# Later places for convolution taps, value-block transposes and LayerNorm in a two-group decoder layer

## The chip, the core and the metric

The kernel runs on one core of one Trainium2 chip. The metric is the device time of one execution in microseconds (us). The core has five engines that work side by side: TensorE (PE in the rows, PEld for its weight loads), VectorE (DVE), ScalarE (ACT), GpSimd (POOL) and SyncE (SP), which issues the transfers. Each engine takes its instructions from its own queue in the order of the program.

## The reference

One layer of a hybrid causal decoder, for a prompt of 2048 tokens and 8 samples of 8 tokens (64 more tokens) that share every weight. Model width 1024, FFN width 2816.

```python
h = RMSNorm(x)
u = h @ w_in      # columns: conf_val 512 | conf_gate 512 | q k v 3*512 | z 512 | beta 4 | a 4
# Conformer group (512 channels): GLU -> causal depthwise conv (31 taps) -> LayerNorm -> swish
# Gated DeltaNet group (4 heads of 128): short conv (4 taps) + SiLU on q, k, v; q and k L2-normed;
#   chunked delta rule (chunks of 64, a triangular solve, then a scan over chunks);
#   per-head RMSNorm * SiLU(z)
x = x + concat(conformer, deltanet) @ w_out
x = x + W_down(SiLU(gate) * val)    # [gate|val] = causal depthwise conv (3) of RMSNorm(x) @ w_up
x = x + (p @ w_ple) * sigmoid(x @ w_ple_gate)
y = RMSNorm(x)
```

The outputs are y for prompt and samples, and the new convolution and delta-rule states of both.

## The kernel before

The tokens are cut into six passes of 2, 3, 3, 3, 3 and 2 tiles of 128 tokens; the last pass carries the 64 sample tokens too. Channels lie on partitions and tokens along the free dimension, so an operation on pass 0 is 128x256 and one on passes 1 to 4 is 128x384. Every weight is split into two parts of a shorter number format, so that each block of a product is three matmuls (`gemm`, PE rows `g<-hT,w`, `g<-mx,w`, `g<-fbuf,w`).

The work is written as a list of units, each with a place (a number), and the list is sorted by place. `units_b` makes the units of the mixing half of a pass: `conf_gate` (GLU of one channel block, with a tanh of ScalarE, row `t<-g`, that reads the projection's accumulator), the convolution taps (31 per block of 128 channels, each one VectorE multiply-add, rows `cacc<-H,cfS,cacc`), `dn_block(j)` (projection, short conv and SiLU of one q, k or v block; j from 8 to 11 are the four value blocks; its last operation is the VectorE row `y<-t,y`, on a tanh of ScalarE, `t<-y`), `dn_tail(j)` (for a value block: transposes of y on TensorE, rows `m<-ident,y`, and a VectorE product with `irk`), `z_block`, the inversion of the triangular blocks (VectorE rows `tv` and `H<-H,tv`; its `tv` and every tanh take turns in the same three buffers `t`), the scan over chunks (`v_new`, `state`, then `out_a` and `out_b`), LayerNorm (`ln_a`, `ln_b`) and `swish`. `units_mx` splits the mixed result into its two parts (rows `mx<-H`, `mx<-zs`) for the product with w_out.

Passes 0 and 1 share the blocks of w_in: their units are sorted together in the joint stage (about 0 to 293 us), whose places run from 0 to 28 and come from `joint_places`. The rest of the mixing of pass 1 lies beside the FFN of pass 0. From then on, the mixing of pass p+1 lies beside the FFN of pass p: `merge` threads its units, at the fractions 0 to 1 that `usual_places` gives, through those of `units_f` (rows of `gate` and `val` read hT, rows of `down` read fbuf). The FFN of passes 1, 2, 3 and 4 runs at 746 to 1200, 1282 to 1716, 1798 to 2236 and 2318 to 2755 us; each is followed by the product with w_out (`proj`) of the pass after it.

The list is not the last word. A scheduler takes the units in the order of the list, plays them against a timeline of its own, and writes the order of each engine's queue. Where an instruction stands is therefore read from the queues, and not from the places.

Helpers hide the callers' lines in the rows: L89 is every matmul, L93 every transpose, L96 every multiply-add with a per-partition scalar, L100 and L102 operations with a scalar, L105 operations on two tensors, L108 every ScalarE operation.

Of the kernel before, what the change touches and what calls it, by code (L numbers as in the profile page):

```python
# [42 lines left out]
def step_kernel(  # L43
# [36 lines left out]
    def gbank():  # L80
        return pg.tile([P, 512], F32, tag="g", name=nm("g"))
# [25 lines left out]
    def act(out, in_, f=AF.Copy, **kw):  # L107
        A.activation(out, in_, f, **kw)  # L108
# [38 lines left out]
    def r_tile(tag, w=NMAX, dt=F32):  # L147
        return rp.tile([P, w], dt, tag=tag, name=nm(tag), bufs=3)

    def srow_tile():  # L150
        return rp.tile([P, NSQ, 38], F32, tag="srow", name=nm("srow"), bufs=2)
# [275 lines left out]
    def units_b(q, pl):  # L427
# [9 lines left out]
        def take(key):  # L437
            if second and key in hold:
                return hold.pop(key)
            w = get()  # L440
            if first and key not in alone:
                hold[key] = w
            return w

        def add(place, f, *keys):
            out.append((place, keys, f))
# [2 lines left out]
            pass  # L449

        z = St()

        def sm(tag, last=H):
            return dp.tile([P, NG, last], F32, tag=tag, name=nm(tag), bufs=2 if tag in LIVE else 1)
# [35 lines left out]
        def dn_block(j):  # L490
            dnS, qk = W["dn"], z.qk
            w = take(("w_in", D + j * P))
            row = r_tile("row", NMAX + 3)
            y = qk[:, 4 + j if j < 4 else j - 4, :] if j < 8 else r_tile("y")
            srow = srow_tile() if sam else None
            G.tensor_copy(row[:, 0:3], dnh[:, j, 0:3])
            if sam:
                G.tensor_copy(srow[:, :, 0:3], dnS[:, j, 4:28].rearrange("p (s r) -> p s r", r=3))
            ps = gbank()
            gemm_w(ps[:, :n], w, q.hT, 0, n)  # L500
            to_row(q, row, srow, 3, ps, lambda o, i, *a: act(o, i))
            act(y[:, :n], ps[:, :n], scale=dnS[:, j, 3:4])
            G.tensor_copy(dnh[:, j, 0:3], row[:, np_:np_ + 3])
            if sam:
                G.tensor_copy(dnh[:, j, 3:27].rearrange("p (s r) -> p s r", r=3), srow[:, :, 8:11])
            for tap in (2, 1, 0):
                for o, i in taps(q, y, row, srow, tap):
                    stt(V, o, i, dnS[:, j, tap:tap + 1], o, MUL, ADD)
            th = t_tile()
            act(th[:, :n], y[:, :n], AF.Tanh)  # L510
            stt(V, y[:, :n], th[:, :n], 1.0, y[:, :n], ADD, MUL)
            if j >= 8:
                z.y = y

        def dn_tail(j):
            if j < 8:
                y = z.qk[:, 4 + j if j < 4 else j - 4, :]
                ss = z.ssq if j < 4 else z.ssk
                ps = bank()
                sq = t_tile("sq")  # L520
                act(sq[:, :n], y[:, :n], AF.Square)
                for t, c0, L in tiles:
                    mm(ps[:L, t:t + 1], sq[:, c0:c0 + L], one1[:, 0:1], t == 0, t == len(tiles) - 1)
                V.tensor_copy(ss[:, 0:nt, j % 4], ps[:, 0:nt])
                if sam:
                    V.tensor_copy(ss[:NSAM, nt:nt + 1, j % 4], ps[:NSAM, nt:nt + 1])
            else:
                h, y = j - 8, z.y
                ps = bank()
                for t in range(nt):  # L530
                    trn(ps[:, t * P:(t + 1) * P], y[:, t * P:(t + 1) * P])
                tt(V, z.vtk[:, 0:nt, h * P:(h + 1) * P], ps[:, :nt * P].rearrange("p (t c) -> p t c", c=P),
                   bc(z.irk[:, 0:nt, h], P, 2), MUL)
                if sam:
                    ps = bank()
                    trn(ps[:NSAM, :P], y[:, np_:n])
                    ts(V, z.vts[:, h * P:(h + 1) * P], ps[:NSAM, :P], z.irk[:NSAM, nt, h:h + 1], MUL)
# [511 lines left out]
        for (what, j), p in pl.at.items():  # L1049
            if what == "cv":  # L1050
                add(p, lambda j=j: conf_val(j), *keys("w_in", j * P))
            elif what == "cg":
                add(p, lambda j=j: conf_gate(j), *keys("w_in", CW + j * P))
            elif what == "dn":
                add(p, lambda j=j: dn_block(j), *keys("w_in", D + j * P))
                add(p + pl.tail, lambda j=j: dn_tail(j))
            elif what == "z":
                add(p, lambda j=j: z_block(j), *keys("w_in", 2560 + j * P))
        spread(staged(units[0] + units[1], [decay]), *pl.decay)
# [16 lines left out]
        if sam:  # L1076
            p = pl.smp
# [15 lines left out]
    def usual_places(g0, g1):  # L1093
        pl = Places()
        seq = [("cv", 3), ("cg", 3), ("dn", 4), ("cv", 0), ("cg", 0), ("dn", 5), ("dn", 6), ("cv", 1), ("cg", 1),
               ("dn", 7), ("cv", 2), ("cg", 2)] + [("dn", j) for j in (0, 1, 2, 3, 8, 9, 10, 11)] + [
                   ("z", h) for h in range(H)]
        dg = (g1 - g0) / len(seq)
        pl.begin = g0 - 0.02
        pl.at = {("ba", 0): g0 - 0.019}  # L1100
        pl.at.update({k: g0 + dg * i for i, k in enumerate(seq)})
        dn = [pl.at["dn", j] for j in range(12)]
        pl.tail = 0.9 * dg
        pl.soft, pl.eg = g0 + 0.01, g0 + 0.03
        pl.decay = (g0 + 0.05, dn[5])
        pl.k_norm = [dn[j] + 1.3 * dg for j in (5, 7)]
        pl.gram_k = [(dn[j] + 1.6 * dg, dn[j] + 2.6 * dg) for j in (5, 7)]
        pl.gram_q = [(dn[j] + 1.6 * dg, dn[j] + 2.6 * dg) for j in (1, 3)]
        pi = dn[7] + 2.7 * dg
        pl.inv = (pi, pi + 0.03, pi + 0.15)  # L1110
        pl.q_norm = dn[3] + 2.7 * dg
        p = pl.at["cg", 3] + dg
        cuts = [p + (0.86 - p) * x for x in (0, 0.2, 0.42, 0.70, 1.0)]
        pl.conv = [(b, max(cuts[i], pl.at["cg", b] + dg), cuts[i + 1]) for i, b in enumerate((3, 0, 1, 2))]
        pl.smp = dn[3] + 2.8 * dg
        pl.scan = (max(g1 + 0.01, pi + 0.19), 0.965)
        pl.ln, pl.swish = (0.87, 0.92), (0.925, 0.96)
        return pl

    def joint_places(second):  # L1120

        pl = Places()
        seq = [("ba", 0)] + [("dn", j) for j in (4, 5, 6, 7)] + [("cv", 1), ("cg", 1)] + [
            ("dn", j) for j in (8, 9, 10, 11)] + [("cv", 2), ("cg", 2)] + [("dn", j) for j in (0, 1, 2, 3)] + [
                ("z", h) for h in range(H)]
        own = [("cv", 3), ("cg", 3), ("cv", 0), ("cg", 0)]
        lag = 0.4 if second else 0.0
        pl.at = {k: 4 + i + lag for i, k in enumerate(seq)}
        pl.at.update(zip(own, (25, 26, 27, 28) if second else (0, 1, 2, 3)))
        pl.begin = 3.8 if second else -0.5  # L1130
        pl.tail = 0.9
        pl.soft, pl.eg = 5.5 + lag / 2, 6.0 + lag / 2
        pl.k_norm = [7.3 + lag, 9.2 + lag]
        if second:
            pl.decay = (100.0, 100.07)
            pl.gram_k = [(100.03, 100.09), (100.09, 100.14)]
            pl.gram_q = [(100.16, 100.22), (100.22, 100.28)]
            pl.inv = (100.145, 100.18, 100.32)
            pl.q_norm = 100.3
            pl.conv = [(b, 100.14 + 0.17 * i, 100.31 + 0.17 * i) for i, b in enumerate((1, 2, 3, 0))]  # L1140
            pl.scan = (100.36, 100.965)
            pl.ln, pl.swish = (100.85, 100.91), (100.915, 100.95)
        else:
            pl.decay = (6.3, 8.5)
            pl.gram_k = [(7.6, 8.6), (9.5, 10.5)]
            pl.inv = (10.7, 11.7, 16.5)
            pl.gram_q = [(19.6, 20.6), (21.6, 22.6)]
            pl.q_norm = 22.7
            pl.conv = [(3, 2.0, 7.0), (0, 7.0, 12.0), (1, 12.0, 17.0), (2, 17.0, 22.0)]
            pl.scan = (17.6, 27.5)  # L1150
            pl.ln, pl.swish = (22.3, 25.0), (25.0, 26.5)
        return pl


# [249 lines left out]
    def even(units, p0, p1):  # L1404
        return [(p0 + (p1 - p0) * i / len(units), *u) for i, u in enumerate(units)]

    u0, u1 = units_b(ps_[0], joint_places(False)), units_b(ps_[1], joint_places(True))
    joint = u0 + [u for u in u1 if u[0] < 49] + even(units_a(ps_[1]), 0.1, 3.8) + [(1.6, (), small)]
    um = units_mx(ps_[0])
    joint += even(um[0:4], 26.6, 27.4) + even(um[4:8], 27.6, 28.4) + [(22.8, (), load_ffn)]  # L1410
    joint.sort(key=lambda u: u[0])
    plan = units_a(ps_[0]) + [u[1:] for u in joint]
    for ip, q in enumerate(ps_):
# [17 lines left out]
        else:  # L1431
            back = [(u[0] - 100, *u[1:]) for u in u1 if u[0] >= 100.14] if prev is None else units_b(
                nxt, usual_places(0.04, 0.55))
            um = units_mx(nxt)
# [36 lines left out]
```

## Time and profile before

| | us |
|---|---|
| median of 3 runs | 3140.59 |
| lowest, highest | 3140.39, 3149.44 |
| the profiled execution | 3149.25 |
| its span, first to last instruction | 3147.5 |

The mean granted clock of TensorE was 0.974 of full speed. In the rows, busy time is the time in which an engine worked; the idle time before an instruction has behind it the work that ended the wait. The profiled execution is one near the highest of the three times.

### The profile page before, as it was taken

The numbers are of one execution on the slowest core, as the hardware profiler recorded it, in microseconds if no ns is written. First come the engines' busy times: TensorE is split into PE (matmuls) and PEld (weight loads), VectorE is DVE, ScalarE is ACT, GpSimd is POOL, SyncE is SP. The second block draws the span as 40 slices with busy tenths as digits, with TensorE's granted clock in tenths as the row PEclk, the third lists the DMA queues.
The fourth block names the chain that finished last, engine by engine and source line by source line (L and its number), as shares of the span: only waits on it lengthen the run. The fifth ranks groups of instructions, "written<-read, shape, count | busy, mean of one in ns | idle before, by whom it ended". The sixth has DMA issues, their size and how long they took to land.

```text
span 3147.5 us, 50438 instructions
## 1 busy us (share of the span) xinstructions
PE 2966.5 (94%) x18418; PEld 2886.3 (92%) x18418; DVE 2144.5 (68%) x5378; ACT 1093.1 (35%) x2440; POOL 810.3 (26%) x1485
## 2 busy tenths in 40 slices
PE   5979889787999999999999999999999999998998
PEld 5979788787998999999999999999999999998998
DVE  6996889756778685668557656857577866743444
ACT  3434334434232443422234332233342222423223
POOL 3422454334323431311111211111131211111221
PEclk8989899888999999999999999999999999998999
DMA  7646788587777767666756677665767775666886
GB/s 229 200 131 203 241 253 249 191 289 271 259 248 248 256 232 253 248 240 237 244 202 225 227 255 248 233 227 199 253 239 256 259 241 199 224 231 227 293 297 215
DMA packets 300414, 745.25 MB, mean 237 GB/s; under 512 B 51241, under 2 KB 213546, under 8 KB 225023
## 3 DMA queue, kind: packets, MB, share of 16 engines
q1 hardware_dynamic: 300167, 742.03, 69.1%
q8 instruction: 146, 2.39, 0.3%
q14 instruction: 101, 0.83, 0.1%
HBM read 607.75 MB, written 134.57 MB: 236 GB/s over the span
## 4 chain that ended last, share of the span: by engine, by line
PE 63%; DVE 8%; DMA 5%; ACT 1%; issue 1%; SPq 0%; POOL 0%; DVEq 0%; ACTq 0%; POOLq 0%
PE g L89 56%; PE d L89 3%; DMA w<-halves 3%; PE m L89 2%; DVE h L96 1%; PE d L93 1%; DVE y L96 1%; PE m L93 1%; DVE cacc L96 1%; DVE X L100 0%; DVE hT L105 0%; DVE rt L105 0%; DVE H L96 0%; DVE tv L105 0%; DVE zs L105 0%
## 5 line engine op out<-in xcount | busy, mean ns | idle before, releaser
L89 PE MATMUL g<-hT,w 128*128 128x384 f32 (+2 forms) x9048 | 1580.3, 332 | 35.6 <-DMA w<-halves 11.9
L89 PEld LDWEIGHTS g<-hT,w 128*128 128x128 f32 x9048 | 1499.4, 191 | 44.9 <-ACT hT L108 10.8
L89 PE MATMUL g<-fbuf,w 128*128 128x384 f32 (+2 forms) x2904 | 534.9, 334 | 21.8 <-ACT w L108 8.4
L96 DVE SCALAR_TENSOR_TENSOR y<-row,ffS,y 128x384 f32<-128x384 f32 (+1 forms) x528 | 321.5, 609 | 296.5 <-ACT y L108 271.3
L89 PEld LDWEIGHTS g<-fbuf,w 128*128 128x128 f32 x2904 | 477.9, 189 | 31.5 <-DVE X L105 11.2
L96 DVE SCALAR_TENSOR_TENSOR cacc<-H,cfS,cacc 128x384 f32<-128x384 f32 (+1 forms) x696 | 452.8, 651 | 10.6 <-ACT cacc L108 3.7
L105 DVE TENSOR_TENSOR X<-X,g 128x384 f32<-128x384 f32 (+2 forms) x532 | 277.3, 525 | 238.6 <-PE g L89 236.4
L108 ACT ACTIVATE row<-g 128x384 f32<-128x384 f32 (+1 forms) x336 | 152.7, 455 | 640.7 <-PE g L89 639.2
L105 POOL TENSOR_TENSOR w<-raw,w 128x1024 fp32r<-128x1024 f32 x90 | 223.9, 2488 | 183.9 <-ACT w L108 169.8
L1237 POOL COPY ffh<-row 128x2 f32<-128x2 f32 x264 | 57.7, 218 | 638.2 <-ACT row L108 633.3
L89 PE MATMUL g<-x,w 128*128 128x384 f32 (+2 forms) x1152 | 201.7, 328 | 5.7 <-ACT w L108 4.4
L89 PE MATMUL g<-mx,w 128*128 128x384 f32 (+2 forms) x1152 | 193.9, 328 | 9.7 <-DMA w<-halves 8.7
L89 PEld LDWEIGHTS g<-mx,w 128*128 128x128 f32 x1152 | 187.8, 192 | 11.3 <-issue 4.8
L89 PEld LDWEIGHTS g<-x,w 128*128 128x128 f32 x1152 | 189.7, 193 | 6.5 <-ACT w L108 4.8
L1230 POOL COPY row<-ffh 128x2 f32<-128x2 f32 x264 | 79.9, 303 | 432.0 <-DVE y L96 328.6
L108 ACT ACTIVATE y<-g,ffS 128x384 f32<-128x384 f32 (+2 forms) x264 | 169.1, 641 | 0.0
L105 POOL TENSOR_TENSOR fbuf<-y,fbuf 128x384 fp32r<-128x384 f32 (+2 forms) x132 | 135.2, 1024 | 110.8 <-ACT fbuf L108 108.7
L108 ACT ACTIVATE fbuf<-y 128x384 fp32r<-128x384 f32 (+2 forms) x132 | 65.8, 498 | 213.0 <-DVE y L105 212.7
L89 PE MATMUL g<-hf,w 128*128 128x256 f32 x528 | 128.0, 398 | 10.9 <-DMA w<-in_w_up_dram 7.1
L108 ACT ACTIVATE w<-raw 128x1024 fp32r<-128x1024 f32 x106 | 112.0, 1056 | 55.0 <-PE g L89 24.2
L108 ACT ACTIVATE y<-y 128x384 f32<-128x384 f32 (+2 forms) x132 | 65.7, 498 | 187.0 <-DVE y L96 186.5
L89 PEld LDWEIGHTS g<-hf,w 128*128 128x128 f32 x528 | 103.7, 202 | 26.1 <-issue 4.4
(344 smaller groups left out, 3384.2 us busy)
## 6 DMA issues: line engine op xcount, KB each, us to landing
w<-halves SPq DMA_DIRECT2D x477, 1024.0 KB
halves<-w SPq DMA_DIRECT2D x106, 1024.0 KB
raw<-in_w_up_dram SPq DMA_DIRECT2D x44, 512.0 KB
w<-in_w_up_dram SPq DMA_DIRECT2D x33, 512.0 KB
raw<-in_w_in_dram SPq DMA_DIRECT2D x24, 512.0 KB
raw<-in_w_down_dram SPq DMA_DIRECT2D x22, 512.0 KB
xt<-in_x_prompt_dram SPq DMA_DIRECT2D x16, 512.0 KB
xT<-xt SPq DMA_DIRECT2D x16, 512.0 KB
```

The lines of the kernel that those rows point to most:

```text
L89: T.matmul(out, lhsT=lhsT, rhs=rhs, start=start, stop=stop, skip_group_check=skip)
L93: T.transpose(out, in_, ident[:k, :k])
L96: return e.scalar_tensor_tensor(out=out, in0=in0, scalar=scalar, in1=in1, op0=op0, op1=op1)
L105: e.tensor_tensor(out=out, in0=a, in1=b, op=op)
L108: A.activation(out, in_, f, **kw)
L1230: G.tensor_copy(row[:, 0:2], ffh[:, col, 0:2])
L1237: G.tensor_copy(ffh[:, col, 0:2], row[:, np_:np_ + 2])
```

## The change

Three sets of places are other numbers, and one variable becomes a dictionary. No instruction is added or taken away.

```diff
         z = St()
+        z.y = {}
...
             if j >= 8:
-                z.y = y
+                z.y[j] = y
...
-                h, y = j - 8, z.y
+                h, y = j - 8, z.y.pop(j)
...
                 add(p, lambda j=j: dn_block(j), *keys("w_in", D + j * P))
-                add(p + pl.tail, lambda j=j: dn_tail(j))
+                add(p + (pl.tail if j < 8 else pl.vtail), lambda j=j: dn_tail(j))
...
-        pl.tail = 0.9 * dg
+        pl.tail, pl.vtail = 0.9 * dg, 1.4 * dg
...
-        cuts = [p + (0.86 - p) * x for x in (0, 0.2, 0.42, 0.70, 1.0)]
+        cuts = (0.25, 0.43, 0.58, 0.72, 0.86)
...
-        pl.tail = 0.9
+        pl.tail, pl.vtail = 0.9, 1.3
...
-            pl.conv = [(3, 2.0, 7.0), (0, 7.0, 12.0), (1, 12.0, 17.0), (2, 17.0, 22.0)]
+            pl.conv = [(3, 2.0, 8.0), (0, 8.0, 13.5), (1, 13.5, 19.0), (2, 19.0, 24.0)]
...
-            pl.ln, pl.swish = (22.3, 25.0), (25.0, 26.5)
+            pl.ln, pl.swish = (24.2, 26.2), (26.2, 27.2)
...
-    joint += even(um[0:4], 26.6, 27.4) + even(um[4:8], 27.6, 28.4) + [(22.8, (), load_ffn)]
+    joint += even(um[0:4], 27.2, 28.0) + even(um[4:8], 28.0, 28.6) + [(22.8, (), load_ffn)]
```

Three places in the queues show what becomes of it.

VectorE in the joint stage, between the SiLU products of the last two value blocks (`y_315` of pass 0 and `y_323` of pass 1 before, `y_314` and `y_322` in the changed kernel; the rows begin behind the first of them and end with the second). Before:

```order
L105 TENSOR_TENSOR H2_33_255<-H2_33_255,tv_308_1804 128x17x15
L96 SCALAR_TENSOR_TENSOR cacc_276_1623<-H2_33_255,cfS_457,cacc_276_1623 128x256
L105 TENSOR_TENSOR tv_318_1857<-H2_33_255 128x256
L105 TENSOR_TENSOR H2_33_255<-m_329_1923,irk_38_260 128x2x128
L96 SCALAR_TENSOR_TENSOR cacc_276_1623<-H2_33_255,cfS_457,cacc_276_1623 128x256
L105 TENSOR_TENSOR H2_33_255<-H2_33_255,tv_318_1857 128x256
L105 TENSOR_TENSOR tv_319_1860<-H2_33_255 128x240
L105 TENSOR_TENSOR H2_33_255<-H2_33_255,tv_319_1860 128x240
L96 SCALAR_TENSOR_TENSOR cacc_276_1623<-H2_33_255,cfS_457,cacc_276_1623 128x256
L105 TENSOR_TENSOR tv_321_1870<-H2_33_255 128x224
L96 SCALAR_TENSOR_TENSOR cacc_276_1623<-H2_33_255,cfS_457,cacc_276_1623 128x256
L96 SCALAR_TENSOR_TENSOR y_323_1874<-t_325_1907,y_323_1874 128x384
```

In the changed kernel:

```order
L105 TENSOR_TENSOR H2_33_255<-H2_33_255,tv_308_1796 128x17x15
L105 TENSOR_TENSOR tv_317_1843<-H2_33_255 128x256
L105 TENSOR_TENSOR H2_33_255<-H2_33_255,tv_317_1843 128x256
L105 TENSOR_TENSOR tv_318_1846<-H2_33_255 128x240
L105 TENSOR_TENSOR H2_33_255<-H2_33_255,tv_318_1846 128x240
L96 SCALAR_TENSOR_TENSOR cacc_304_1780<-H2_33_255,cfS_457,cacc_304_1780 128x256
L105 TENSOR_TENSOR tv_320_1855<-H2_33_255 128x224
L96 SCALAR_TENSOR_TENSOR cacc_304_1780<-H2_33_255,cfS_457,cacc_304_1780 128x256
L105 TENSOR_TENSOR H2_33_255<-m_337_1956,irk_38_260 128x2x128
L96 SCALAR_TENSOR_TENSOR y_322_1859<-t_324_1892,y_322_1859 128x384
```

Of the four taps (`cacc`) between the two products two are left. Counted from the start of the queue, 75 taps of pass 0 stand ahead of the second product before and 65 in the changed kernel; of every other kind of VectorE work as much stands ahead as before.

TensorE at the end of the FFN of pass 1, from the last `state` matmuls of pass 2's scan (`d_2099`, `d_2100`) on; `d_2116` and `d_2117` are its last `out_b`, `g_2097` the last `val` product, `g_2105` and on the `down` products. Before:

```order
L89 MATMUL d_2099_11939<-S_131,H2_1414_7693 128x128 x2
L89 MATMUL d_2100_11942<-vn_2088_11878,ke_2090_11883 128x128 x2
L89 MATMUL d_2099_11939<-vn_2088_11878,DT_1415_7694 128x128
L93 MATMUL m_2078_11816<-ident_83,ln_2065_11741 128x128 x4
L89 MATMUL d_2099_11939<-vn_2088_11878,DT_1415_7694 128x128
L89 MATMUL g_2105_11972<-fbuf_1406_7651,w_2079_11822 128x384 x6
L89 MATMUL g_2106_11980<-fbuf_1406_7651,w_2079_11822 128x384 x6
```

The `out_b` of the same chunk stands further on, behind 14 `down` products of six matmuls each:

```order
L89 MATMUL g_2125_12105<-fbuf_1406_7651,w_2111_12016 128x384 x6
L89 MATMUL g_2126_12113<-fbuf_1406_7651,w_2111_12016 128x384 x6
L93 MATMUL d_2116_12050<-ident_83,on_2085_11868 128x128 x2
L93 MATMUL d_2117_12054<-ident_83,on_2101_11949 128x128 x2
L89 MATMUL g_2127_12121<-fbuf_1406_7651,w_2111_12016 128x384 x6
```

In the changed kernel:

```order
L89 MATMUL d_2099_11939<-S_131,H2_1414_7693 128x128 x2
L89 MATMUL d_2099_11939<-vn_2088_11878,DT_1415_7694 128x128 x2
L93 MATMUL m_2058_11719<-ident_83,ln_2037_11602 128x128 x4
L89 MATMUL d_2100_11942<-vn_2088_11878,ke_2090_11883 128x128 x2
L93 MATMUL m_2067_11743<-ident_83,H2_1414_7693 128x128 x4
L89 MATMUL g_2097_11902<-hT2_1251_6951,w_2071_11769 128x384 x2
L93 MATMUL d_2116_12050<-ident_83,on_2085_11868 128x128 x2
L93 MATMUL d_2117_12054<-ident_83,on_2101_11949 128x128 x2
L93 MATMUL m_2078_11816<-ident_83,ln_2065_11741 128x128 x4
L93 MATMUL m_2157_12412<-ident_83,pt_2156_12410 128x128 x2
L89 MATMUL g_2097_11902<-hT2_1251_6951,w_2071_11769 128x384 x22
L89 MATMUL g_2105_11972<-fbuf_1406_7651,w_2079_11822 128x384 x6
```

The last `out_b` has moved ahead of 22 of the 24 `val` matmuls and of all `down` products; between the `d_2099` that it needs and itself stand four transposes of `ln_b` (`m_2058`), two matmuls `d_2100`, four transposes of `ln_a` (`m_2067`) and two matmuls of `val`. Two transposes that stood in this place before (`d_2089` of `v_new` and `d_2091` of `out_b`) now stand behind 22 matmuls of `gate`.

TensorE at the end of the FFN of pass 2; `m_2875` is the last `ln_b` of pass 3's LayerNorm, `d_2913` and `d_2914` its last `out_b`, `g_2929` the first product with w_out. Before (behind the last row shown follow 12 more `down` products, then the first twelve matmuls of `g_2929`, then `d_2913` and `d_2914`):

```order
L89 MATMUL g_2903_17280<-fbuf_2302_13116,w_2876_17122 128x384 x6
L93 MATMUL m_2875_17116<-ident_83,ln_2865_17046 128x128 x4
L89 MATMUL d_2896_17239<-S_131,H2_2307_13153 128x128 x2
L89 MATMUL d_2897_17242<-vn_2885_17178,ke_2887_17183 128x128 x2
L89 MATMUL d_2896_17239<-vn_2885_17178,DT_2308_13154 128x128 x2
L89 MATMUL g_2904_17288<-fbuf_2302_13116,w_2876_17122 128x384 x6
L89 MATMUL g_2905_17296<-fbuf_2302_13116,w_2876_17122 128x384 x6
```

In the changed kernel:

```order
L89 MATMUL g_2920_17391<-fbuf_2302_13116,w_2901_17270 128x384 x6
L93 MATMUL m_2875_17116<-ident_83,ln_2865_17046 128x128 x4
L93 MATMUL m_2954_17712<-ident_83,pt_2953_17710 128x128 x2
L93 MATMUL d_2913_17350<-ident_83,on_2882_17168 128x128 x2
L93 MATMUL d_2914_17354<-ident_83,on_2898_17249 128x128 x2
L89 MATMUL g_2922_17405<-fbuf_2302_13116,w_2908_17316 128x384 x6
L89 MATMUL g_2923_17413<-fbuf_2302_13116,w_2908_17316 128x384 x6
L89 MATMUL g_2924_17421<-fbuf_2302_13116,w_2908_17316 128x384 x6
L93 MATMUL m_2956_17719<-ident_83,pt_2955_17717 128x128 x2
L89 MATMUL g_2925_17429<-fbuf_2302_13116,w_2908_17316 128x384 x6
L93 MATMUL d_3011_17967<-ident_83,xt_3002_17940 128x128 x4
L89 MATMUL g_2929_17448<-mx_2915_17358,w_2916_17365 128x384
```

`ln_b` has moved from 14 to four `down` products ahead of the first product with w_out, and `out_b`, which stood behind the first twelve matmuls of that product, stands with it. The end of the FFN of pass 3 changes alike.

## Rows read from the trace of the kernel before

**Rows 1.** The page: busy time of each engine, share of the span, instructions.

```profile
PE 2966.5 (94%) x18418; PEld 2886.3 (92%) x18418; DVE 2144.5 (68%) x5378; ACT 1093.1 (35%) x2440; POOL 810.3 (26%) x1485
```

**Rows 2.** Stretches: length; busy us (instructions) of PE, PEld, DVE, ACT, POOL; clock; DMA.

```profile
80.00:150.00 70.00, 69.94 (x493) 69.40 (x492) 69.54 (x220) 28.61 (x62) 28.77 (x37) 1.00 0.64 198
...
170.00:180.00 10.00, 1.28 (x5) 0.70 (x5) 9.83 (x22) 1.40 (x2) 2.48 (x1) 0.73 0.83 249
180.00:190.00 10.00, 2.63 (x12) 2.63 (x13) 9.66 (x34) 0.88 (x2) 0.42 (x2) 0.50 0.00 0
190.00:200.00 10.00, 10.00 (x67) 10.00 (x67) 7.88 (x18) 4.15 (x9) 4.77 (x15) 0.91 0.20 27
...
240.00:290.00 50.00, 50.00 (x374) 48.96 (x373) 26.10 (x91) 18.65 (x50) 4.24 (x6) 1.00 0.46 153
```

**Rows 3.** Waits of TensorE, 150 to 190 us: total us, times, longest.

```profile
PE m L93 <- DVE y L96: 11.6, 5, 4.2
```

**Rows 4.** TensorE by time: start, length, operation, idle before and its releaser.

```profile
173.86 0.41 PE L93 MATMUL m<-ident,y 128*128 128x128 f32 x2 [4.12 <-DVE y L96]
178.43 0.87 PE L93 MATMUL m<-ident,y 128*128 128x128 f32 x3 [4.16 <-DVE y L96]
187.37 2.93 PE L89 MATMUL g<-hT,w 128*128 128x256 f32 x12 [8.06 <-ACT t L108]
```

**Rows 5.** VectorE by time, 148 to 190 us.

```profile
160.57 0.42 DVE L96 SCALAR_TENSOR_TENSOR y<-t,y 128x256 f32<-128x256 f32 x1
...
171.15 2.56 DVE L96 SCALAR_TENSOR_TENSOR y<-t,y 128x256 f32<-128x256 f32 x1
...
177.34 0.48 DVE L96 SCALAR_TENSOR_TENSOR cacc<-H,cfS,cacc 128x256 f32<-128x256 f32 x1
177.74 0.55 DVE L96 SCALAR_TENSOR_TENSOR y<-t,y 128x384 f32<-128x384 f32 x1
```

**Rows 6.** ScalarE by time, 165 to 190 us.

```profile
186.94 0.38 ACT L108 ACTIVATE t<-g 128x256 f32<-128x256 f32 x1 [10.48 <-DVE H L105]
```

**Rows 7.** GpSimd by time, 150 to 182 us.

```profile
170.96 2.48 POOL L105 TENSOR_TENSOR w<-raw,w 128x1024 fp32r<-128x1024 f32 x1 [14.36 <-ACT w L108]
```

**Rows 8.** Stretches, as rows 2: the FFN of passes 1 and 2.

```profile
746.00:1200.00 454.00, 432.11 (x2551) 423.46 (x2552) 328.80 (x686) 169.01 (x338) 157.95 (x217) 0.98 0.76 260
...
1282.00:1716.00 434.00, 431.81 (x2627) 426.76 (x2626) 290.74 (x717) 145.27 (x317) 77.67 (x191) 1.00 0.67 236
```

**Rows 9.** Waits of TensorE in the FFN of pass 1: total, times, longest.

```profile
PE g L89 <- DMA w<-halves: 11.2, 5, 3.6
```

**Rows 10.** TensorE by time, 1170 to 1183 us, end of the FFN of pass 1.

```profile
1174.18 0.44 PE L93 MATMUL d<-ident,H 128*128 128x128 f32 x2 [1.86 <-DVE S L96]
1175.19 0.69 PE L93 MATMUL d<-ident,on 128*128 128x128 f32 x2 [0.57 <-DVE vn L105]
...
1181.79 0.39 PE L89 MATMUL d<-vn,DT 128*128 128x128 f32 x2
```

**Rows 11.** TensorE by time, 1196 to 1202 us.

```profile
1198.37 0.60 PE L93 MATMUL d<-ident,on 128*128 128x128 f32 x4
```

**Rows 12.** ScalarE by time, a scan tail in the FFN of pass 2.

```profile
1672.66 0.39 ACT L108 ACTIVATE on<-d 128x256 f32<-128x256 f32 x1 [3.17 <-PE d L89]
```

**Rows 13.** VectorE by time, the same scan tail.

```profile
1678.14 0.87 DVE L100 TENSOR_SCALAR on<-on,so 128x128 f32<-128x128 f32 x4
```

**Rows 14.** TensorE by time, end of the FFN of pass 2.

```profile
1698.77 0.60 PE L93 MATMUL m<-ident,ln 128*128 128x128 f32 x4
...
1704.07 11.89 PE L89 MATMUL g<-fbuf,w 128*128 128x384 f32 x66
...
1721.22 8.57 PE L89 MATMUL g<-mx,w 128*128 128x384 f32 x48
```

**Rows 15.** ScalarE by time, end of the FFN of pass 2.

```profile
1699.40 0.60 ACT L108 ACTIVATE H<-m 128x512 f32<-128x512 f32 x1 [1.35 <-PE m L93]
...
1709.27 0.53 ACT L108 ACTIVATE mx<-H 128x384 fp32r<-128x384 f32 x1 [1.51 <-DVE H L96]
```

## The prediction

> **What bounds the kernel now.** I read the busy times first: TensorE works in 94% of the span, VectorE in 68% [rows 1]. So a change of order can pay only where TensorE waits, and the next view is the table of stretches. In the joint stage TensorE is full from 80 to 150 us and from 240 to 290, but between 170 and 190 it works 3.9 us of 20, while VectorE works 19.5 of them [rows 2]. The chain of single rows says how: the transposes of the value blocks wait for the SiLU product y of VectorE, 11.6 us in five waits [rows 3], the longest two 4.12 and 4.16 us; then the next projection stands 8.06 us until a tanh of the GLU has read an accumulator [rows 4]. That tanh of ScalarE runs at 186.94, released by an inversion step of VectorE [rows 6], since the inversion and the tanh take turns in three buffers. Both waits have one cause: VectorE is behind, and between the products it works on convolution taps of 0.48 us [rows 5]. In the usual passes it is otherwise. The FFN of pass 2 has TensorE busy in 431.81 of 434 us [rows 8], and VectorE 291, so there is nothing to win. The FFN of pass 1 loses some 22 us, of which 11.2 are waits for weights that come by DMA [rows 9], which taps don't touch.
>
> **Joint stage, value blocks: a gain of 4.5 us.** The queue of VectorE has 65 taps instead of 75 ahead of the last value product, and nothing else differs there. Ten taps of 0.48 us [rows 5] are 4.8 us. The value tails themselves hardly move on TensorE, as the scheduler leaves them behind their y; so the gain is that of the taps, not of the later tails. It is passed on: the last transposes wait for that y, the tanh for a later step of the same queue, so TensorE restarts about 4.8 us before 187.37 [rows 4]; from there it is full in the stretches shown, up to 290 [rows 2], and what it starts earlier it ends earlier. Not all ten taps were in TensorE's way: one or two of those moved lay ahead of 75 us, and the step that frees the buffer needs its predecessors too. I take 4.5, not under 3. The upper bound: the product y of 171.15 takes 2.56 us, its like at 160.57 takes 0.42 [rows 5]; the long one runs while GpSimd splits weights, 170.96 to 173.44 [rows 7]. If it comes clear of that, a further 2.1, together 6.9.
>
> The Trainium skill says on this in GPSIMD Engine Reference, Key points, that GpSimd shares its SBUF interfaces with VectorE and that VectorE operations with two SBUF inputs contend with it. The rows agree, 2.56 against 0.42. By that rule the 2.1 us are only passed on to whatever stands beside the split, a tap for instance, and the sum would be 4.5 or 6.6 according to which of the two is hit.
>
> **Joint stage, its end: a loss of 1 us.** The ten taps, LayerNorm, swish and the split come later. VectorE has 24 us free between 240 and 290 [rows 2], and 4.8 us of taps lie in them. TensorE needs the swish and its split at the product with w_out at 293 us. From `ln_b` to the last split of swish ScalarE took 10.4 us in another pass (1699.40 to 1709.80) [rows 15]. Swish now ends at place 27.2 where it ended at 26.5, and the product follows at 28.6; a place is some 10 us (28 in 293), so 1.4 places are 14 us, enough if ScalarE does little else, and 2 too few if it does half as much again. Between nothing and 2; I take 1.
>
> **End of the FFN of pass 1: a loss of 4 us.** Two transposes that waited 1.86 and 0.57 us [rows 10] now have 22 matmuls of `gate` ahead of them, so 2.4 us go. But the last `out_b`, which stood at 1198.37, 16 us behind the `state` matmuls of 1181.79 [rows 10, 11], now has only ten transposes and small matmuls and two of `val` between, 1.9 us by these rows' lengths (0.15 us each, 0.2 for `val`). What it waits for: `on<-d` on ScalarE, the scale chain, `on<-on,so`. Where this chain ran with little between, it took from 1672.66 [rows 12] to 1679.01 [rows 13], 6.35 us. So TensorE stands 4.5 us at the least; behind it in the queue stand `val` and all of `down`, which nobody can take forward. At the most the third tile of LayerNorm, which now shares VectorE's queue with the chain, and ScalarE's other work (`ln_b` 0.6 us [rows 15], its like for LayerNorm and a `gate`) add 4.8: 9.3. Less 2.4 that is a loss of 2 to 7. I take 4, a little under the middle, since the chain that I took for the lower bound already had LayerNorm steps among its own.
>
> After the wait of 8.06 us the granted clock was 0.50 in 180 to 190 and 0.91 in 190 to 200, where it had been 1.00 [rows 2]: half, 1.2 GHz, until TensorE had been busy again. Twelve matmuls of 2.93 us [rows 4] ran at that level, so a wait of that length can cost up to 1.5 us more. I leave it out of the sum: a wait of 4.5 us is nearer to that of 4.16 than to that of 8.06.
>
> **Ends of the FFN of passes 2, 3 and 4: a loss of 4 us.** `ln_b` had 14 `down` products behind it before the first product with w_out, it now has four; 66 matmuls of `down` take 11.89 us from 1704.07 on [rows 14], so 4 products are 4.3 us, and with `out_b` and transposes of 0.15 us each 5.9. ScalarE needs 10.4 us from `ln_b` to the last split [rows 15], and its queue now has seven more operations in between (four splits of `out_b`, two squares, a copy of p): half a us each by the same rows, 3.7, together 14.1. TensorE can fill with the part of the product that doesn't need the last blocks, 30 of the 72 matmuls that the scheduler threads together; at 0.18 us (48 in 8.57) [rows 14] 5.4. So 11.3 against 10.4 to 14.1: between nothing and 3 us at each of two ends, 1.5 each. At the third, which ends with the samples' chain, the same bounds; I take 1.
>
> **Inside the usual passes: nothing.** The first taps move from a tenth of the pass to a quarter. TensorE doesn't wait there in passes 2 to 4 [rows 8]; the cover for the later taps is VectorE's free third, and if that is gone at the end, the last two parts already hold the price.
>
> Sum: -4.5 + 1 + 4 + 4 = +4.5. The profiled execution took 3149.25 us, near the highest of the three times; carried to it this is 3153.7. Carried to the median, 3140.6, it is 3145.
>
> **The rivals.** *Faster: the joint stage gives more, the ends cost nothing.* A gain of 6.9 at the value blocks, and at the end of pass 1 the chain is as fast as its best row while 2.4 us of old waits go; the three ends stay hidden under 11.3 us of other work. If the DMA waits of pass 1 shift by luck as well, about -12: 3128. For it speaks that VectorE's queue decides 19.7 us of TensorE's waits [rows 3, 4]; against it that every other part of the change moves work towards the end of a full pass.
>
> *Slower: the ends stall.* One mechanism: `ln_b` and the scan's last `out_b` stand close ahead of the product with w_out, and ScalarE's chain from `ln_b` is longer than TensorE's work behind it. It decides from 11.3 us on. At 14.1 and a little more for interleaved work, 3 to 4 us at three ends, 7 at the end of pass 1, 2 in the joint stage, less 4.5: +15, 3156. For it: ScalarE's 10.4 us have only some 1.5 us of idle time in them [rows 15], so more operations lengthen them. Against: the scheduler put them there by its own timeline, and part of the product needs no late block.
>
> *Nothing is moved that matters.* The tails of the value blocks stay where they were, TensorE is the bound, and gains and losses are each under 3 us: 3141. The Trainium skill points that way, Perfetto Trace Analysis, Identifying the Most-Contended Engine: improvement comes from the engine with the highest occupancy. The rows of the usual passes agree with it, 431.81 us of 434 for TensorE; by it alone the time would be that of before, less the joint stage's gain. With my forecast it makes one case in what can be measured.
>
> **The numbers.** Two medians of this kernel less than 0.3% (9.4 us) apart can't be told from no change. Within it, with my forecast and with the quiet rival: 0.45. The stalls: 0.30. More gain: 0.25. Range 3128 to 3158, from the faster rival's end to a little over the slower one's; the likeliest case alone is 3134 to 3150.
>
> **What would show it.** Right: TensorE's wait for a tanh of about 8 us still there in the joint stage, ending near 182.5 instead of 187.4; at the end of the FFN of pass 1 a new wait of 4 to 9 us ahead of transposes `d<-ident,on`, with the two waits for S and vn gone; waits of up to 3 us ahead of `g<-mx,w` at the ends of passes 2 and 3; the passes' middles unchanged. Wrong: the joint stage's waits gone rather than shifted, or no wait ahead of `out_b`, or a wait of over 5 us at each pass's end.

## The result, and the profile after

The changed kernel takes 3166.82 us in the median (3166.27 to 3171.92) where the kernel before takes 3140.49 beside it: a ratio of 1.0075 [1.0058, 1.0091]. By the medians it is 26 us slower, by the ratio 24. The prediction was 3145 with a range up to 3158. The profiled execution has a span of 3170.2 us, 22.7 more than before.

The page, busy times of the changed kernel:

```profile
PE 2978.8 (94%) x18418; PEld 2896.4 (91%) x18418; DVE 2146.2 (68%) x5378; ACT 1093.2 (34%) x2440; POOL 808.3 (25%) x1485
```

The instructions are as many as before [rows 1]. Of the 22.7 us TensorE is busy in 12.3 (the mean granted clock is 0.971 where it was 0.974; 0.3% of 2979 us are 9) and idle in 10.4. Where they came in is read best by following single matmuls. The table gives, at times of the kernel before, how much later (us) the same matmul starts than in the profiled execution of before (median of 15 matched matmuls around the time). The last five columns are kernels of the experiments further down.

| at, in before | after | e5 | e12 | e8 | e7 | e10 |
|---|---|---|---|---|---|---|
| 290, end of the joint stage | -1.1 | -0.3 | -1.3 | 1.2 | 0.2 | 1.9 |
| 746, start of the FFN of pass 1 | -2.0 | -1.8 | 3.8 | -1.1 | -1.0 | -4.1 |
| 1140 | 2.2 | 1.2 | 7.8 | 3.2 | 3.2 | -1.8 |
| 1230, behind its end | 8.5 | 6.3 | 9.2 | 9.9 | 3.0 | -3.6 |
| 1850, FFN of pass 3 | 9.4 | 7.0 | 10.2 | 10.2 | 4.9 | -4.7 |
| 2225, ahead of its end | 9.2 | 7.0 | 9.7 | 8.9 | 5.7 | -4.9 |
| 2350, behind it | 18.4 | 12.1 | 17.9 | 13.3 | 6.2 | -4.2 |
| 3100 | 22.1 | 18.3 | 23.8 | 20.9 | 10.3 | -0.5 |

In `after` the loss comes in four steps: 4.2 us inside the FFN of pass 1, 6.3 at its end, 9.2 at the end of the FFN of pass 3, 3.7 behind it. The profiled execution of before was 8.7 us above its median and that of the changed kernel 5.1 above its own, so the table says where, and the ratios say how much.

**Joint stage.** Waits of TensorE, 150 to 190 us, after:

```profile
PE g L89 <- ACT t L108: 10.3, 1, 10.3
PE m L93 <- DVE y L96: 4.3, 2, 3.2
```

TensorE by time, after (start, length, operation, idle before and its releaser):

```profile
186.19 9.04 PE L89 MATMUL g<-hT,w 128*128 128x256 f32 x50 [10.31 <-ACT t L108]
...
297.57 0.63 PE L93 MATMUL d<-ident,on 128*128 128x128 f32 x3 [2.39 <-DVE on L100]
...
334.16 0.58 PE L89 MATMUL g<-hT,w 128*128 128x256 f32 x1 [1.02 <-ACT hT L108]
```

The last of these, the first product of the FFN of pass 0, before:

```profile
330.87 0.58 PE L89 MATMUL g<-hT,w 128*128 128x256 f32 x1 [1.02 <-ACT hT L108]
```

VectorE by time, after:

```profile
170.31 0.42 DVE L96 SCALAR_TENSOR_TENSOR y<-t,y 128x256 f32<-128x256 f32 x1
...
174.67 0.55 DVE L96 SCALAR_TENSOR_TENSOR y<-t,y 128x384 f32<-128x384 f32 x1
...
175.55 2.40 DVE L105 TENSOR_TENSOR tv<-H 128x208 f32<-128x208 f32 x1
...
294.01 2.31 DVE L105 TENSOR_TENSOR rt<-rt,rx 128x4 f32<-128x4 f32 x1
```

GpSimd by time, after:

```profile
175.29 2.43 POOL L105 TENSOR_TENSOR w<-raw,w 128x1024 fp32r<-128x1024 f32 x1 [16.61 <-ACT w L108]
...
293.93 2.37 POOL L105 TENSOR_TENSOR w<-raw,w 128x1024 fp32r<-128x1024 f32 x1
```

The waits for y fall from 11.6 us [rows 3] to 4.3, and the last y comes 3.1 us earlier (174.67 for 177.74 [rows 5]). But the wait for the tanh grows from 8.06 to 10.31, and TensorE restarts at 186.19 where it restarted at 187.37 [rows 4]: 1.2 us are left. The y of 2.56 us [rows 5] is short now, and the inversion step `tv` beside GpSimd's split takes 2.40 in its place; the tanh waits for that chain. So most of the 3.1 us is not the taps' own: the first of the two y begins only 0.84 us earlier (170.31 for 171.15 [rows 5]), and 2.14 are its own length (0.42 for 2.56), which `tv` takes back. Of the ten taps' 4.8 us about 1 reached the value products; where the rest went was not followed further.

At 294.01 it happens again: an operation on 128x4 elements, of which the neighbours take 0.16, takes 2.31 beside a split of 2.37, and `out_b` behind it waits 2.39. At 290 us TensorE was still 1.1 us ahead of before (the table's first row), and the FFN of pass 0 begins 3.3 us later than before (334.16 for 330.87): the end of the joint stage loses some 4.4 us, 2.39 of them in that wait.

**End of the FFN of pass 1.** TensorE, then ScalarE, then VectorE, after:

```profile
1185.23 1.01 PE L89 MATMUL g<-hT,w 128*128 128x384 f32 x2 [6.84 <-ACT w L108]
1186.04 1.05 PE L93 MATMUL d<-ident,on 128*128 128x128 f32 x4
```

```profile
1184.12 1.06 ACT L108 ACTIVATE w<-raw 128x1024 fp32r<-128x1024 f32 x1 [4.03 <-DMA raw<-in_w_up_dram]
```

```profile
1182.81 0.68 DVE L100 TENSOR_SCALAR on<-on,so 128x128 f32<-128x128 f32 x3
```

SyncE's queue (issue times), after, and then that of before:

```profile
1173.35 5.43 SPq L1309 DMA_DIRECT2D row<-in_w_ple_dram  x2
1178.88 0.42 SPq L253 DMA_DIRECT2D raw<-in_w_up_dram  x1
```

```profile
1159.13 1.42 SPq L253 DMA_DIRECT2D raw<-in_w_up_dram  x1
```

Waits of SyncE's queue, 1165 to 1200 us, after (total us, times, longest):

```profile
SPq L1309 <- DVE y L96: 10.5, 3, 4.6
```

The granted clock behind the stall (stretch, busy us of PE, PEld, DVE, ACT, POOL, clock, DMA), after, and then before:

```profile
1186.00:1200.00 14.00, 14.00 (x80) 13.86 (x79) 10.63 (x21) 12.75 (x29) 4.54 (x5) 0.86 0.93 333
```

```profile
1186.00:1200.00 14.00, 13.93 (x80) 13.02 (x78) 13.84 (x39) 9.14 (x23) 5.58 (x8) 1.00 0.93 352
```

The stall of 6.84 us is there, but it stands two matmuls ahead of `out_b`, and a weight ends it: the load of the last `val` block was issued 19.8 us later than before. It stands behind two loads of w_ple (L1309), and these waited for VectorE's work on y. Underneath lies the predicted chain: the last `on` ends at 1183.49, 5.1 us after TensorE ran dry at 1178.4. The two matmuls of `val` ahead of `out_b` would have filled 0.4 us of that, so with this order of TensorE's queue the chain alone would have stalled it some 4.7 us (an estimate), and the weight adds some 2. Behind the stall the granted clock was 0.86 where before it was 1.00; over 14 us that is some 2 us more (an estimate from these two rows).

**Ends of the FFN of passes 2 and 3.** SyncE's queue at the end of pass 2, after and before:

```profile
1720.33 0.33 SPq L1293 DMA_DIRECT2D pt<-in_p_prompt_dram  x1
1720.75 3.86 SPq L370 DMA_DIRECT2D xt<-in_x_prompt_dram  x2
1725.33 0.33 SPq L250 DMA_DIRECT2D w<-halves  x1
```

```profile
1699.44 0.33 SPq L1292 DMA_DIRECT2D pt<-in_p_prompt_dram  x1
...
1703.25 1.42 SPq L370 DMA_DIRECT2D xt<-in_x_prompt_dram  x2
1707.53 8.78 SPq L250 DMA_DIRECT2D w<-halves  x3
```

TensorE at these two ends and, in the last five rows, at the end of the FFN of pass 4, after:

```profile
1719.65 0.60 PE L93 MATMUL m<-ident,ln 128*128 128x128 f32 x4
1720.09 0.38 PE L93 MATMUL m<-ident,pt 128*128 128x128 f32 x2
...
1726.59 0.63 PE L93 MATMUL d<-ident,xt 128*128 128x128 f32 x4 [1.29 <-DMA xt<-in_x_prompt_dram]
...
1731.55 11.37 PE L89 MATMUL g<-mx,w 128*128 128x384 f32 x64 [1.41 <-DMA w<-halves]
...
2248.41 0.63 PE L93 MATMUL d<-ident,xt 128*128 128x128 f32 x4 [1.95 <-DMA xt<-in_x_prompt_dram]
...
2254.90 20.34 PE L89 MATMUL g<-mx,w 128*128 128x384 f32 x105 [3.60 <-DMA w<-halves]
...
2771.22 0.56 PE L89 MATMUL g<-mx,w 128*128 128x320 f32 x2 [1.15 <-ACT mx L108]
...
2772.48 1.15 PE L89 MATMUL g<-mx,w 128*128 128x320 f32 x6 [0.33 <-POOL mx L105]
2773.56 3.78 PE L89 MATMUL d<-vz,kes 64*128 64x512 f32 x4
...
2777.34 3.53 PE L89 MATMUL g<-mx,w 128*128 128x320 f32 x13
...
2788.56 1.68 PE L89 MATMUL g<-mx,w 128*128 128x320 f32 x9 [0.88 <-ACT mx L108]
```

No wait for ScalarE is to be seen at the ends of passes 2 and 3; TensorE waits for x and for weights. Tiles of LayerNorm (`ln`), of p, of x and of raw weights take turns in three buffers (`xio` in the kernel). In this order the third tile of p takes the buffer that the last `ln` leaves, and x takes those of p. The last `ln_b` transposes began at 1719.65 and ended at 1720.25, and the third load of p was issued at 1720.33; before, they ended at 1699.37 [rows 14] and the load was issued at 1699.44. So it comes 21 us later, by the late `ln_b`. The load of x waits for the transposes of p, which moved along behind `ln_b`, and the weights of w_out stand behind x in SyncE's queue. At the end of pass 4 the waits are for `mx`, as the prediction had it.

Stretches, after: length, busy us of PE, PEld, DVE, ACT, POOL, clock, DMA.

```profile
180.00:190.00 10.00, 3.81 (x19) 3.81 (x20) 9.59 (x36) 0.88 (x2) 0.73 (x2) 0.52 0.35 99
190.00:200.00 10.00, 10.00 (x73) 9.96 (x72) 8.34 (x17) 4.73 (x11) 6.39 (x19) 1.00 0.26 51
...
746.00:1200.00 454.00, 428.63 (x2505) 419.93 (x2505) 329.23 (x680) 165.98 (x337) 154.24 (x213) 0.97 0.74 253
1282.00:1716.00 434.00, 432.11 (x2625) 427.35 (x2624) 289.66 (x723) 139.28 (x308) 75.75 (x193) 1.00 0.67 231
2770.00:2780.00 10.00, 8.52 (x26) 5.38 (x26) 9.26 (x14) 7.21 (x20) 7.71 (x7) 0.68 0.50 158
```

### The profile page after: what moved, and what is told of

It is laid out like the page before. It is cut to its first block, busy times and chain, and to the rows that moved or that the text cites. A ratio compares the mean times of both kernels' runs of the same rounds, so it can differ in the third digit from the quotient of the medians.

```text
span 3170.2 us, 50434 instructions
## 1 busy us (share of the span) xinstructions
PE 2978.8 (94%) x18418; PEld 2896.4 (91%) x18418; DVE 2146.2 (68%) x5378; ACT 1093.2 (34%) x2440; POOL 808.3 (25%) x1485
## 3 DMA queue, kind: packets, MB, share of 16 engines
q8 instruction: 146, 2.39, 0.3%
## 4 chain that ended last, share of the span: by engine, by line
PE 62%; DVE 8%; DMA 5%; ACT 1%; issue 1%; SPq 0%; POOL 0%; ACTq 0%; DVEq 0%; POOLq 0%
PE g L89 56%; DMA w<-halves 3%; PE d L89 3%; PE m L89 2%; DVE h L96 1%; DVE y L96 1%; PE d L93 1%; PE m L93 1%; DVE cacc L96 1%; DMA raw<-in_w_up_dram 1%; DVE hT L105 0%; DVE X L105 0%; DVE sy L96 0%; DVE zs L105 0%; DVE X L100 0%
## 5 line engine op out<-in xcount | busy, mean ns | idle before, releaser
L89 PE MATMUL g<-hT,w 128*128 128x384 f32 (+2 forms) x9048 | 1582.5, 332 | 42.5 <-ACT t L108 10.3
L89 PEld LDWEIGHTS g<-fbuf,w 128*128 128x128 f32 x2904 | 480.3, 190 | 31.9 <-DVE X L105 10.4
```

The costliest lines, as they stand in the source:

```text
L89: T.matmul(out, lhsT=lhsT, rhs=rhs, start=start, stop=stop, skip_group_check=skip)
```

## The experiments

The first four part the change. Ratios are to the kernel before in the same comparison, with 95% intervals; its median moved between 3140.5 and 3148.6 us from one comparison to the next, so the ratios count and not the medians.

**e1**: only the new cuts of the taps in the usual passes, on the kernel before.

```diff
-        cuts = [p + (0.86 - p) * x for x in (0, 0.2, 0.42, 0.70, 1.0)]
+        cuts = (0.25, 0.43, 0.58, 0.72, 0.86)
```

> Of the change only the later taps of the usual passes (the cuts 0.25, 0.43, 0.58, 0.72, 0.86). The delay of matched matmuls against before grows by about 7, 3, 7 and 7 us at the ends of the FFN of passes 1, 2, 3 and 4, and nowhere else for good. If the cuts alone make these stalls, this kernel takes about 3164 us (before plus 24), with the joint stage as before. Rival: the stalls come of the joint stage's new order, which shifts every later transfer; then the cuts alone stay within 5 us of 3140.

Measured: 1.0054 [1.0034, 1.0073], 3169.56 us. The cuts alone bring a loss of this size; the interval overlaps that of the whole change.

**e2**: the changed kernel with the old line of cuts.

> The whole change with the cuts of the usual passes put back. If the cuts carry the loss, what is left is the joint stage with its tails: 1 to 5 us faster than before, 3136 to 3140, with TensorE's restart after the tanh earlier. Rival (joint stage to blame): 3155 or more.

Measured: 0.9999 [0.9987, 1.0011], 3147.64 us. The rest of the change does nothing that can be measured. Its trace has the wait of 2.4 us ahead of `out_b` in the joint stage.

**e3**: only the joint stage's places of taps, LayerNorm, swish and splits, on the kernel before.

> Of the change only the joint stage's later taps, LayerNorm, swish and split; tails and cuts as before. If the ten taps fewer ahead of the last value product are what moves TensorE's restart in the joint stage, this has the same joint stage as the whole change (the product with w_out starts 1 us earlier than before) and takes 3137 to 3141. Rival: the later tails matter too, then the product with w_out starts no earlier than before, 3140 or a little more.

Measured: 1.0016 [1.0004, 1.0028], 3153.16 us. Its trace has the joint stage of the changed kernel: the tanh waits 10.3 us, y 4.3 in two waits, the slow `tv` at 175.42 for 2.40 us, the 2.4 ahead of `out_b`. So the gain at the value blocks is lost to the joint places themselves, not to another part. As a whole they cost a little, where a gain was expected.

**e4**: only the later value tails, on the kernel before.

```diff
+        z.y = {}
-                z.y = y
+                z.y[j] = y
-                h, y = j - 8, z.y
+                h, y = j - 8, z.y.pop(j)
-                add(p + pl.tail, lambda j=j: dn_tail(j))
+                add(p + (pl.tail if j < 8 else pl.vtail), lambda j=j: dn_tail(j))
-        pl.tail = 0.9 * dg
+        pl.tail, pl.vtail = 0.9 * dg, 1.4 * dg
-        pl.tail = 0.9
+        pl.tail, pl.vtail = 0.9, 1.3
```

> Of the change only the later places of the value-block tails, in the joint stage and in the usual passes. The queue of TensorE hardly changes by it, so 3140 within 3 us. Rival: holding two value blocks at once lets TensorE go on with a projection instead of a transpose, and some of the 11.6 us of waits for y go: 3132 to 3136.

Measured: 0.9992 [0.9982, 1.0002], 3147.16 us. Nothing that can be told.

**e5, e6**: one buffer for the tiles of p of a pass in place of one each, so that p takes one turn in the three buffers and not three, and the first two loads of x no longer wait for p's transposes; on the changed kernel (e5) and on that before (e6).

```diff
+            pts = xio("pt")
...
-                pt = xio("pt", (P, 256))
+                pt = pts[:, t * 256:(t + 1) * 256]
```

> The changed kernel, with the three tiles of p of a pass in one buffer of the ring that p, x and raw weights share, instead of one each. TensorE's order at the ends of passes 2 and 3 stays that of the changed kernel (last LayerNorm transposes and out_b four down products ahead of the product with w_out). Theory 1 (transfers): p's tiles wait in that ring for late transposes, x waits behind them in SyncE's queue and the weights of the product with w_out behind x; then the waits for xt and w there (1.3 and 1.4 us, 1.9 and 3.6) shrink to under 1 and the delay added at these two ends falls from 3 to 4 and 7 us to 1 or 2 each; in all some 3158. Theory 2 (as predicted, ScalarE's chain from the LayerNorm to the splits): the delays stay, with waits for mx in place of those for transfers, 3166.

> The kernel before with the same edit of p's tiles, as the control: if the ring isn't short there, 3140 within 4 us, and nothing new at the ends of the passes.

Measured: e5 1.0055 [1.0037, 1.0074], 3164.42 us; e6 0.9980 [0.9970, 0.9989], 3141.16. Waits of TensorE in e5, end of the FFN of pass 3 (those of pass 2 read the same):

```profile
PE g L89 <- ACT mx L108: 2.1, 1, 2.1
```

The waits for x and weights are gone, so the buffers and the queue had been their cause. What was hidden under them appears: the wait for ScalarE's split that the prediction had named, 2.1 us. The step at the end of pass 3 falls from 9.2 to 5.1. The whole time shows less: the interval of e5 overlaps that of the changed kernel, and the buffer helps the kernel before as well, by 0.2% (its matmuls start 6 us earlier already at 746, not at the ends). Against e6, e5 loses 0.75%, as much as the changed kernel against that before. So the buffers explain the waits at these ends, and not the loss as a whole.

**e7, e8**: which half of the cuts. e7 is the changed kernel with its late start of the taps and about the old last stretch; e8 is the kernel before with its early start and the new last stretch.

```diff
+        cuts = (0.25, 0.37, 0.50, 0.627, 0.86)      # e7
+        cuts = (0.0825, 0.238, 0.409, 0.72, 0.86)   # e8
```

> The changed kernel with cuts 0.25, 0.37, 0.50, 0.627, 0.86: the taps start as late as in the change, the last block has the stretch that it had before. If the late start of the taps costs the time, 3160 or more. If it is the last block alone, whose 31 taps are pressed into 0.72 to 0.86 and push LayerNorm back, the ends are as before and this takes what the change without the cuts took: 3140 within 4 us, with no new delay at the pass ends.

> The kernel before with only the last cut changed: 0.0825, 0.238, 0.409, 0.72, 0.86. If the last block's stretch alone makes the loss, this shows all of it: 7, 3 to 5, 7 and 5 to 7 us at the ends of the FFN of passes 1 to 4, 3158 to 3165, although the taps start as early as before. If the late start matters, 3140 to 3145.

Measured: e7 1.0026 [1.0015, 1.0036], 3154.76 us; e8 1.0068 [1.0051, 1.0086], 3168.26 us. The last stretch alone, 31 taps in 0.14 of a pass in place of 0.233, brings nearly the whole loss. In e8 the steps at the ends of passes 1 and 3 are there (6.7 and 4.4 us); in e7 they are gone (-0.2 and 0.5), and its 0.26% come in the middle of pass 1 and behind 2350.

**e9, e10**: is it the density of the last taps, or that they end late? e9 begins the last stretch in between; e10 has the new density but ends earlier. Both on the kernel before.

```diff
+        cuts = (0.0825, 0.238, 0.409, 0.67, 0.86)   # e9
+        cuts = (0.0825, 0.238, 0.409, 0.66, 0.80)   # e10
```

> The kernel before with the last cut at 0.67, between the 0.627 of before and the 0.72 of the change. In the queue of TensorE the last LayerNorm transposes then stand 72 matmuls ahead of the product with w_out (84 before, 24 in the change) and p's transposes 54 (66 and 6). If the loss comes when they get too near to that product, there is little of it here: 3141 to 3148, waits under 1 us at the ends of passes 2 and 3. If it grows in step with the cut, 43% of the way, 3150 to 3155.

> The kernel before with cuts 0.0825, 0.238, 0.409, 0.66, 0.80: the last block's taps lie as dense as in the change (0.14 of a pass), but end 0.06 of a pass (26 us) sooner. If the loss is that the last taps are done too late for what follows them, it is gone: within 5 us of before. If the density itself costs (VectorE overloaded, everything else on it late), the loss is there: 3158 to 3168.

Measured: e9 0.9997 [0.9986, 1.0009], 3146.61 us; e10 1.0012 [1.0002, 1.0022], 3150.04. The same density is nearly free when it ends at 0.80, so it is lateness that counts. The last tap beside the FFN of pass 2, and the first product with w_out, begin at 1665 and 1716 us before, at 1671 and 1719 in e9, 1646 and 1714 in e10, 1669 and 1720 in e7, but at 1685 and 1727 in the changed kernel and 1685 and 1728 in e8. The loss doesn't grow in step with the cut: 0.67 is free and 0.72 costs 0.7%. What lies between was not tried.

**e12**: the changed kernel, with the last block of `gate` and the last of `val` split already in pass 0, so that pass 1 reads them as halves and not as raw weights.

```diff
-        if key[0] == "w_up" and key[1] // P % 4 and key not in seen:
+        if key[0] == "w_up" and key[1] // P % 4 and key[1] // P not in (21, 43) and key not in seen:
```

> The changed kernel, with the last gate and the last val block of w_up split in the FFN of pass 0 already, so that pass 1 loads them whole and its end needs no raw weight. If the wait of 6.8 us at the end of the FFN of pass 1 is that for the raw weight, it goes, and the delay added there falls from 7 to 3 or 4 us (what the end of pass 2 shows), at a price of up to 2 us in the FFN of pass 0: 3160 to 3164. If the scan's chain ahead of the last out_b makes it, a wait of about 5 us ahead of d<-ident,on takes its place and the time stays at 3166.

Measured: 1.0082 [1.0064, 1.0100], 3172.47 us. Waits of TensorE in e12 at the end of pass 1, 1130 to 1230 us, the longest two:

```profile
PE g L89 <- DMA w<-halves: 1.3, 1, 1.3
PE d L93 <- DMA xt<-in_x_prompt_dram: 1.2, 1, 1.2
```

TensorE by time in e12:

```profile
1188.43 12.03 PE L89 MATMUL g<-fbuf,w 128*128 128x384 f32 x68
...
1200.95 0.60 PE L93 MATMUL d<-ident,on 128*128 128x128 f32 x4
```

The wait of 6.84 us is gone, and the step from 1140 to 1230 falls from 6.3 to 1.4. But the edit changed two things: no raw weight is loaded there, and the scheduler put the last `out_b` back behind 72 `down` matmuls, 68 of them in this row (84 stood ahead of it before the change, none in the changed kernel). So this run doesn't part the late weight from the `out_b` chain; only the times above do, some 4.7 us for the chain and 2 more for the weight. The kernel doesn't win by it, since splitting early costs 5.8 us in the FFN of pass 0 (3.8 for -2.0 at 746).

**e11**: what is left as useful: the kernel before with e6's buffer and e4's tails.

> The kernel before with p's tiles in one buffer and the value-block tails later, without any of the other places: the two edits that were not slower by themselves (0.9980 and 0.9992 of before). If their gains add up, 0.997 of before, some 3138 against 3147; if they are one and the same gain or chance of order, 0.998 to 0.999.

Measured: 0.9969 [0.9959, 0.9980], 3137.76 us where the kernel before took 3148.58 beside it. The two gains add up, as expected. It is ahead of both kernels; ahead of that before by 0.31%, about the 0.3% that the prediction took as the least that can be told.

## Why the prediction was wrong

The sign of the ends was foreseen, and their size was not; the gain set against them didn't come. Two terms failed most: the value blocks' gain, and the ends of passes 2 to 4, where only ScalarE's chain was priced.

- **Value blocks, -4.5: the step that failed is the size.** TensorE restarted 1.2 us earlier, not 4.8. The prediction took ten taps of 0.48 us as time that is passed on whole ("not under 3"). The taps did leave VectorE's queue, but the first of the two last y came only 0.84 us earlier. The last one came 3.1 us earlier because the y before it got clear of GpSimd's split, the 2.1 us that the prediction had as its upper bound. The tanh that TensorE waits for hangs on the inversion, and that took on the slow operation in its place. The prediction named this passing on: when taps leave a queue, the rest of it slides against GpSimd's split, and an operation on the chain can be hit that was clear of it.
- **Joint end, +1 (0 to 2): 4.4, too small and in the wrong place.** From 290 us to the start of the FFN of pass 0 the changed kernel falls from 1.1 us ahead to 3.3 behind. The one large wait there is the same contention at 294.01, 2.39 us ahead of `out_b`, and not a late split of swish. That the whole came out near nothing (e2) is luck: the FFN of pass 0 has waits that took it back, to -2.0 at 746.
- **End of pass 1, +4 (2 to 7): 6.3.** Within the bounds, in part by luck. The predicted chain was there, worth some 4.7 us (4.5 to 9.3 were taken), and the two old waits of 2.4 us went. The weight was later still by some 2, and the lower clock behind the stall, which the prediction left out of its sum, costs some 2. The working counted what the moved units ask of VectorE, ScalarE and TensorE, and not what stands in SyncE's queue.
- **Ends of passes 2 to 4, +4: 13.6 in the table** (8.5 to 22.1), of which 0.7 from the end of pass 2 to that of pass 3, 9.2 at the end of pass 3 and 3.7 behind. The step that failed: ScalarE's chain was taken as the only price. It costs 2.1 us where e5 lays it bare (1.5 was taken, up to 3). The rest at these ends is the buffers that LayerNorm, p and x share: `ln_b` and the transposes of p were among the moved rows that stood ahead of the prediction, and it didn't ask which buffers they hold and which loads stand behind. Of the 9.2 us, 5.3 are idle time of TensorE (2.91 of the 145 us from 2205 on before, 8.21 of the 154 from 2214 on after); the rest is busy time that grew around the waits (the granted clock was 0.91 in 2246 to 2266, where before it was 1.00).
- **Inside the usual passes, nothing: right for passes 2 and 3** (432.11 busy of 434, as [rows 8]), wrong for pass 1, 4.2 us. e7 and e8, with one half of the cuts each, both have it, and e10 has 2.3; e2, with the old cuts, has 0.6. The releasers there are mostly weights as before [rows 9]; what shifts them is open.
- **Rivals.** The slower one was the side, at 3156 still 11 us short, since its mechanism is worth 2.1 us at an end, and the waits for loads were not among the rivals. The quiet one failed: here a pass in which TensorE is full had no slack at its end for work that VectorE, a third idle, does later.

Settled by runs: the cuts are the cause (e1, e2), their last stretch nearly alone (e8), by its lateness (e10); p's turns in the three buffers carry the waits for x and weights (e5). Read from the trace alone: the stall of pass 1, by the `out_b` chain and the late weight together, and the end of pass 4, where waits of 1.15, 0.33 and 0.88 us for `mx` (2.4 together) and the lower clock (some 3.4, worked out below) are more than the 3.7 us of the table. Open: the middle of pass 1, and why 0.67 is free and 0.72 is not.

## What to carry to other kernels

When work is moved later, list for every moved instruction the buffer it frees and the loads that wait for that buffer, and then whatever stands behind those loads in the issuing queue: here the transposes of the last LayerNorm tile, 21 us late, held back p, x and the weights of the next product. Idle share of an engine says nothing on how late its work may be; the distance to the product that needs it does. Taking work out of a queue that runs beside a contending engine can move the collision to another operation, so the gain isn't the length of the work taken out.

## What the hardware showed

In three places a VectorE operation that fell together with GpSimd's split took about that split's time, whatever its own size: 2.56 us for y before [rows 5, 7], 2.40 for `tv`, and 2.31 for 128x4 elements whose neighbours take 0.16. The Trainium skill, SBUF — State Buffer, Who interferes with whom, says that an operation of VectorE with two SBUF inputs contends with a GpSimd instruction that reads SBUF, and that the order of issue, not the shape of the operation, decides which of the two blocks. The rows agree: the three splits took 2.48, 2.43 and 2.37 us and began first.

Behind two short waits at the end of pass 4 (1.15 and 0.33 us) the granted clock fell: it was 0.68 in 2770 to 2780, though TensorE was busy in 8.52 of these 10 us. In the stretch below, after, it was 0.50, the level of 1.2 GHz:

```profile
2774.00:2776.00 2.00, 2.00 (x3) 0.72 (x3) 2.00 (x3) 0.41 (x1) 1.69 (x2) 0.50 0.09 30
```

TensorE ran there four matmuls of 64x512 that took 3.78 us and then 13 of the product with w_out that took 3.53. Before, at a clock of 1.00, the four took 1.98 and 58 of the product 8.75, which is 1.96 for 13; so the clock cost some 1.8 and 1.6 us. Before:

```profile
2753.59 1.98 PE L89 MATMUL d<-vz,kes 64*128 64x512 f32 x4
...
2755.78 8.75 PE L89 MATMUL g<-mx,w 128*128 128x320 f32 x58
```

After a wait of 10.31 us, longer than that of before, the clock was back at 1.00 in 190 to 200, where it had been 0.91 [rows 2]; TensorE had restarted 1.2 us earlier.
